# The first ten microseconds of an encoder layer: how x and the first weights are fetched, and what runs meanwhile

## The chip, the core and the metric

The kernel runs on one core of a Trainium2 chip. A core has engines that work side by side, each through its own list of instructions in order: TensorE (PE in the profile, its weight loads PEld), VectorE (DVE), ScalarE (ACT), GpSimd (POOL) and SyncE (SP). Data come from HBM into the core's SBUF by DMA; here SP and ACT issue transfers, each onto a queue of its own, and 16 DMA engines serve both. The matmuls' results go to PSUM. The metric is the device time of one execution in microseconds, as the median of several runs.

## What is computed

One layer of a hybrid encoder over 256 tokens of 1024 features, in float32: a half feed-forward step, a mixer (attention beside a state space model) and a second half step. Only the beginning of the first half step matters here.

```python
def rmsnorm(x, g):
    xf = x.astype(jnp.float32)
    y = xf * lax.rsqrt(jnp.mean(xf * xf, axis=-1, keepdims=True) + EPS)
    return (y * g).astype(x.dtype)

def swiglu(h, w_gate, w_up, w_down):
    return (jax.nn.silu(h @ w_gate) * (h @ w_up)) @ w_down

x = x + 0.5 * swiglu(rmsnorm(x, ffn1_norm[l]), ffn1_w_gate[l], ffn1_w_up[l], ffn1_w_down[l])
...
x = x + 0.5 * swiglu(rmsnorm(x, ffn2_norm[l]), ffn2_w_gate[l], ffn2_w_up[l], ffn2_w_down[l])
```

`w_gate` and `w_up` are 1024 x 2816, `w_down` is 2816 x 1024.

## The kernel before

x lies in SBUF as 8 tiles of 128 features by 256 tokens. To keep float32 precision with the faster matmul type, every operand is split in two: `hi` is the value rounded to that type (a copy on ACT, L94), and `lo` is the rest (a subtraction on DVE, L97, or L100 where a gain is multiplied in). A product then takes three matmuls: `hi` by `hi`, `hi` weights by `lo` activations, `lo` weights by `hi` activations (`mm3`, L136 to L138).

The half step (`ffn`) runs over 22 blocks of 128 hidden features. A block has 1 MB of weights, half gate and half up, and 2 x 8 x 3 = 48 matmuls of 128x128 weights by 128x256 activations. `wload` fetches weights into one of four `raw` buffers of 512 KB by SP's queue (L117), splits them into `whi` and `wlo` (four buffers each), and lets the splits run ahead of other work by a priority of 50. A planner sorts the instructions of each engine by readiness and priority; after that each engine keeps its order. It gives each transfer one of a fixed set of semaphores, and a transfer whose semaphore is still in use waits on its issuing engine.

The normalisation's factor per token (`R`) is not needed before the matmuls: x times the gain goes in (`Norm.scale`, which writes `xh` and `xl`), and `R` is multiplied in as a block's sum leaves PSUM. `Norm.square` collects the squares of x, and `Norm.finish` makes `R` with two small matmuls, one of which needs the identity matrix in `cst`. PSUM has six buffers for the blocks' sums.

The beginning, in the order of the queues: ACT issues the packed vectors `vec` (with the gains, L165) and then x[2:4] and x[4:8] (L167, L168); SP issues x[0:2] (L166), and behind it block 0's weights in four quarters of 256 KB, then the constants `cst` (L351), the positions and the packed rows (L293, L294), and the weights of block 1. Block 0 is a case of its own: its quarters are split without priority, and its matmuls run gate first (all 8 tiles of x), then up. `hook(f)` is called in each block: at 0 it issues `cst` and makes the squares, at 3 it makes the rotary tables, later it fetches the first weights of the mixer.

Of the kernel before, what the change touches and what calls it, by code (L numbers as in the profile page):

```python
# [15 lines left out]
P = 128  # L16
# [6 lines left out]

# pool depths
RAWB, WB = 4, 4
NMM, NPL, NG = 3, 2, 3
EB, PRB, QKB = 4, 2, 2
# blocks of the first half step during which the mixer's first weights are fetched
PREF = (8, 10, 12, 14, 16, 18)
# how far the splitting of weights runs ahead of other work  # L30
WPRI = 50
# emission order of the mixer, in rounds (one round per group of the state space part):
# attention units, state space units, its norm, weight chunks
A0, DA = -0.0991, 0.1594
# [13 lines left out]

# columns of the packed per-feature vectors
V_F1, V_MIX, V_F2, V_QA, V_KVA, V_SSM, V_DSK, V_CW, V_CB = 0, 8, 16, 24, 27, 29, 45, 61, 181  # L50
V_N = 205
# columns of the packed per-column rows
R_DTB, R_AL, R_GQ, R_GK, R_IF = 0, 64, 128, 224, 320
R_N = 336
# columns of the constant matrices
C_ID, C_TF, C_TB, C_S1, C_S2 = 0, 128, 256, 384, 448
# [16 lines left out]
def build(ctx, tc, A, out, dbg=None):  # L73
# [17 lines left out]

# [1 line left out]
    def copy(dst, src, scale=1.0):  # L93
        S.activation(dst, src, AF.Copy, scale=scale)  # L94

    def tt(dst, a, b, op):
        V.tensor_tensor(out=dst, in0=a, in1=b, op=op)  # L97

# [28 lines left out]
    def split(hi, lo, src, scale=None):  # L127
        if scale is None:
            copy(hi, src)
            tt(lo, src, hi, ALU.subtract)  # L130
        else:
            copy(hi, src, scale)
            stt(lo, src, scale, hi, ALU.mult, ALU.subtract)
# [6 lines left out]
    def wstat(ps, pieces, xh, xl, k0, first, last):  # L140
        """ps[feature, token] += sum over the k tiles held in pieces"""
        ks = [(pc, j) for pc, j0, n in pieces for j in range(j0, j0 + n)]
        for i, (pc, j) in enumerate(ks):
            mm3(ps, pc.hi[:, j * P:(j + 1) * P], pc.lo[:, j * P:(j + 1) * P],
                xh[:, k0 + i], xl[:, k0 + i], first and i == 0, last and i == len(ks) - 1)

    def rsqrt(y, v, n):
        """y = v ** -0.5 on [P, n]"""
        t = sm.tile([P, 8], I32, tag="rs_t", name="rs_t")[:, :n]
        a = sm.tile([P, 8], F32, tag="rs_a", name="rs_a")[:, :n]  # L150
        w = sm.tile([P, 8], F32, tag="rs_w", name="rs_w")[:, :n]
        ts(t, v.bitcast(I32), 1, None, ALU.logical_shift_right)
        ts(y.bitcast(I32), t, -1.0, float(0x5F3759DF), ALU.mult, ALU.add)
        ts(w, v, -0.5, None, ALU.mult)
        for _ in range(3):
            tt(a, y, y, ALU.mult)
            tt(a, a, w, ALU.mult)
            stt(y, a, 1.5, y, ALU.add, ALU.mult)

# [1 line left out]
    vec = cp.tile([P, V_N], F32, name="vec")  # L161
    row = cp.tile([P, R_N], F32, name="row")
    cst = cp.tile([P, C_N], F32, name="cst")
    x = xp.tile([P, KD, T], F32, name="x")
    nc.scalar.dma_start(vec, A["vec"])  # L165
    nc.sync.dma_start(x[:, 0:2], A["xt"][:, 0:2])  # L166
    nc.scalar.dma_start(x[:, 2:4], A["xt"][:, 2:4])  # L167
    nc.scalar.dma_start(x[:, 4:8], A["xt"][:, 4:8])  # L168
    ident = cst[:, C_ID:C_ID + P]
    triF = cst[:, C_TF:C_TF + P]  # L170
    triB = cst[:, C_TB:C_TB + P]
    ones = cp.tile([P, P], F32, name="ones")
    V.memset(ones, 1.0)
    halfpi = cp.tile([P, 1], F32, name="halfpi")
    V.memset(halfpi, PI / 2)

    def token_sums(psp, sq, tag):
        """[token, 2]: the sum of sq[feature, token] over its features"""
        ps = psp.tile([P, 512], F32, tag=tag, name="ps_sum")
        for t in range(2):  # L180
            TE.matmul(ps[:, t:t + 1], sq[:, t * P:(t + 1) * P], ones[:, 0:1], start=True, stop=True)
        return ps[:, 0:2]

    def token_rows(psp, r, tag):
        """[P, token]: r[token, 2] on every partition"""
        dg = sm.tile([P, 2, P], F32, tag="diag", name="diag", bufs=1)
# [18 lines left out]
    class Norm:  # L205
        """x * gain of each tile of x as it comes, and the sum of squares"""

# [27 lines left out]

# [1 line left out]
    def ffn(norm, wgu, wd, after, hook=None):  # L237
        with ExitStack() as es:
# [6 lines left out]
            R = None  # L245
            for f in range(KF):
                ps = ps_mm.tile([P, 2, T], F32, tag="mm", name="ps_gu")
                if f == 0 and hook:
                    pcs = wload(wgu[f], [512], 0)
                    for k in range(KD):  # L250
                        norm.scale(k)
                    pcs += wload(wgu[f, :, 512:2048], [512] * 3, 0)
                    for j in range(2):
                        wstat(ps[:, j], [(pcs[2 * j], 0, 4), (pcs[2 * j + 1], 0, 4)], norm.xh, norm.xl, 0, True, True)
                else:
                    pcs = wload(wgu[f], [1024, 1024])
                    for j in range(2):
                        wstat(ps[:, j], [(pcs[j], 0, KD)], norm.xh, norm.xl, 0, True, True)
                if hook:
                    hook(f)  # L260
                if R is None:
                    R = norm.finish(ps_r, "r")
                gu = ev.tile([P, 2, T], F32, tag="gu", name="gu")
                tt(gu, ps, R.unsqueeze(1).to_broadcast([P, 2, T]), ALU.mult)
                sg = ev.tile([P, T], F32, tag="sg", name="sg")
                S.activation(sg, gu[:, 0], AF.Silu)
                tt(sg, sg, gu[:, 1], ALU.mult)
                split(hh[:, f], hl[:, f], sg)
            for d in range(KD):
                ps = ps_mm.tile([P, 2, T], F32, tag="mm", name="ps_d")  # L270
# [5 lines left out]

# [1 line left out]
    CCq = cp.tile([P, 2, ROPE], F32, name="CCq")  # L278
# [11 lines left out]
    def tables():  # L290
# [6 lines left out]
        V.tensor_copy(eye, ident)  # L297
        # 0 where a pair of tokens counts, -2**100 elsewhere
        ts(msk4[:, 0], ones, 1.0, 2.0 ** 100, ALU.subtract, ALU.mult)
# [42 lines left out]

# [1 line left out]
    n1 = Norm(V_F1)  # L344
# [3 lines left out]

    def hook(f):
        if f == 0:  # L350
            nc.sync.dma_start(cst, A["cst"])  # L351
            for k in range(KD):
                n1.square(k)
        elif f == 3:
            tables()
        elif f in PREF:
# [7 lines left out]

# [1 line left out]
    with ExitStack() as es:  # L366
# [9 lines left out]

# [1 line left out]
        cqh = mp.tile([P, 3, T], F32R, name="cqh")  # L378
# [50 lines left out]

        # rotated shared key and its square sum  # L430
        H = ROPE // 2
# [10 lines left out]

        # dt = softplus(raw + bias), log-decay sums
        u = m0.tile([P, 2, 64], F32, name="dt_u")
# [20 lines left out]
        dump("dt", dt)  # L465
        # log-decay sums counted from the middle of the sequence outwards
        sgt = m0.tile([P, 2, P], F32, name="sgt")
# [36 lines left out]

# [1 line left out]
        def in_group(g):  # L506
# [30 lines left out]

# [1 line left out]
        def attn_group(g):  # L539
            st = {}  # L540

            def proj():
# [4 lines left out]
                for t in range(2):  # L547
# [14 lines left out]
                    copy(kv[:, t], pk, rk[:, t:t + 1])  # L562
                # head norms
                sq = at.tile([P, 512], F32, tag="pr", name="sq", bufs=PRB)[:, :2 * HG * HD].rearrange("p (t h d) -> p t h d", t=2, h=HG)
# [9 lines left out]
                rsqrt(r.rearrange("p a b c -> p (a b c)"), v.rearrange("p a b c -> p (a b c)"), 4 * HG)  # L574
                # rotary part of q, in place
                qr = q4[:, :, :, NOPE:]
# [5 lines left out]
                tt(qr, qr, m2, ALU.add)  # L582
                # k
                ka = at.tile([P, 2, HG, HD], F32, tag="ka", name="ka", bufs=1)
# [52 lines left out]

# [1 line left out]
        def ssd_group(g, xz):  # L639
# [122 lines left out]

# [1 line left out]
        for c in range(4):  # L764
# [24 lines left out]

# [1 line left out]
    ffn(n2, A["w_gu2"], A["w_d2"], lambda d: nc.sync.dma_start(out[:, d], x[:, d]))  # L791


# [1 line left out]
def _tiles(w):  # L795
    """[K, M] -> [M tiles, partition, K tiles, 128]"""
    k, m = w.shape
    return w.reshape(k // P, P, m // P, P).transpose(2, 1, 0, 3)


def _pairs(t):
    """[n, P, K, 128] -> [n / 2, P, 2 * K * 128]"""
    n, p, k, m = t.shape
# [88 lines left out]
```

## Time and profile before

| what | value |
|---|---|
| time, median of 3 runs | 819.84 us (818.7 to 819.92) |
| span of the profiled execution, first to last instruction | 817.6 us |
| TensorE busy in the span | 797.8 us, 6480 matmuls |
| first matmul of block 0 | 7.34 us |
| bytes moved by DMA | 126.61 MB |
| weights of a block, issue to landing | 4.5 us (median of 86 pieces of 512 KB) |
| block 0's quarters, issue to landing | 6.8 us (median of 4 pieces of 256 KB) |

The times are of runs without the profiler; the profile is of one execution, of which it gives the span alone. All stamps below are microseconds from the start of that span. In a row of the timeline the first number is the start and the second the duration of the group, and "x4" counts its instructions. Matmuls are pipelined, so the duration of one is longer than the distance to the next; that distance is what a matmul costs in a row of them.

### The profile page before, as it was taken

How to read it: one execution, taken by the hardware profiler on the slowest of the kernel's cores; microseconds unless marked ns; L12 is line 12 of the kernel's file. 1: busy time of each engine (PE TensorE's matmuls, PEld its weight loads, DVE VectorE, ACT ScalarE, POOL GpSimd, SP SyncE). 2: the span in 40 equal slices, each digit the busy share in tenths (PEclk: the TensorE clock that was granted, in tenths of full speed). 3: DMA queues.
4: the chain of work that ended last, by engine and by line, in shares of the span. 5: the costliest groups of instructions: out<-in, count | busy, mean ns of one | idle time of the engine just before them, and what ended most of it. 6: DMA issues, size and time to landing. Idle time of an engine off the chain costs nothing.

```text
span 817.6 us, 16082 instructions
## 1 busy us (share of the span) xinstructions
PE 797.8 (98%) x6480; PEld 768.8 (94%) x6480; DVE 590.3 (72%) x1192; ACT 470.2 (58%) x810; POOL 0.2 (0%) x4
## 2 busy tenths in 40 slices
PE   6999999999998999999999999999999999999998
PEld 5999999999998998988989999999999999999998
DVE  6977776566797986897897578657787766666543
ACT  6755554455367659679676666557455544444342
POOL 0000000000000000000000000000000000000000
PEclk9999999999999999999999999999999999999999
DMA  7667774667235443322325414342665555554772
GB/s 259 214 212 224 222 229 136 184 184 215 63 92 171 131 131 104 106 79 92 103 85 168 154 52 154 112 146 68 223 184 178 175 184 182 185 184 131 197 206 75
DMA packets 39098, 126.61 MB, mean 155 GB/s; under 512 B 4464, under 2 KB 5872, under 8 KB 39024
## 3 DMA queue, kind: packets, MB, share of 16 engines
q1 hardware_dynamic: 38592, 124.69, 48.7%
q8 instruction: 51, 0.84, 0.4%
q10 hardware_dynamic: 432, 0.89, 0.3%
q14 instruction: 23, 0.19, 0.1%
HBM read 124.52 MB, written 1.05 MB: 154 GB/s over the span
## 4 chain that ended last, share of the span: by engine, by line
PE 86%; DVE 6%; ACT 5%; DMA 2%; issue 1%; ACTq 0%
PE ps_gu L137 10%; PE ps_gu L138 10%; PE ps_gu L136 10%; PE ps_d L136 5%; PE ps_d L137 5%; PE ps_d L138 5%; PE ps_in L137 4%; PE ps_in L138 4%; PE ps_in L136 4%; PE ps_y L690 3%; PE ps_sb L138 2%; PE ps_sb L137 2%; PE ps_sb L136 2%; PE ps_sc L603 2%; PE ps_gt L137 1%; PE ps_o L630 1%
## 5 line engine op out<-in xcount | busy, mean ns | idle before, releaser
L94 ACT ACTIVATE whi<-raw 128x1024 fp32r<-128x1024 f32 (+4 forms) x256 | 251.3, 986 | 209.0 <-PE ps_d L137 53.1
L97 DVE TENSOR_TENSOR wlo<-raw,whi 128x1024 fp32r<-128x1024 f32 (+4 forms) x256 | 289.8, 1134 | 112.1 <-ACT whi L94 111.2
L136 PE MATMUL ps_gu<-xh,whi 128*128 128x256 f32 x704 | 201.0, 285 | 7.9 <-ACT whi L94 7.9
L137 PE MATMUL ps_gu<-xl,whi 128*128 128x256 f32 x704 | 201.2, 286 | 0.5 <-DVE xl L100 0.4
L138 PE MATMUL ps_gu<-xh,wlo 128*128 128x256 f32 x704 | 200.8, 285 | 0.0
L136 PEld LDWEIGHTS ps_gu<-xh,whi 128*128 128x128 f32 x704 | 136.5, 194 | 8.2 <-ACT whi L94 8.2
L137 PEld LDWEIGHTS ps_gu<-xl,whi 128*128 128x128 f32 x704 | 136.5, 194 | 1.0 <-DVE xl L100 0.9
L138 PEld LDWEIGHTS ps_gu<-xh,wlo 128*128 128x128 f32 x704 | 136.4, 194 | 0.5 <-DVE wlo L97 0.5
L137 PE MATMUL ps_in<-xl,whi 128*128 128x256 f32 x368 | 105.3, 286 | 0.1
L138 PE MATMUL ps_in<-xh,wlo 128*128 128x256 f32 x368 | 105.0, 285 | 0.0
L136 PE MATMUL ps_in<-xh,whi 128*128 128x256 f32 x368 | 104.4, 284 | 0.0
L137 PE MATMUL ps_d<-hl,whi 128*128 128x256 f32 x352 | 99.1, 281 | 0.0
L136 PE MATMUL ps_d<-hh,whi 128*128 128x256 f32 x352 | 99.1, 281 | 0.0
L138 PE MATMUL ps_d<-hh,wlo 128*128 128x256 f32 x352 | 99.0, 281 | 0.0
L137 PEld LDWEIGHTS ps_in<-xl,whi 128*128 128x128 f32 x368 | 70.1, 191 | 0.6 <-DVE xl L100 0.3
L138 PEld LDWEIGHTS ps_in<-xh,wlo 128*128 128x128 f32 x368 | 70.1, 191 | 0.5 <-issue 0.3
L136 PEld LDWEIGHTS ps_in<-xh,whi 128*128 128x128 f32 x368 | 70.1, 191 | 0.1
L136 PEld LDWEIGHTS ps_d<-hh,whi 128*128 128x128 f32 x352 | 66.3, 188 | 0.0
L137 PEld LDWEIGHTS ps_d<-hl,whi 128*128 128x128 f32 x352 | 66.3, 188 | 0.0
L138 PEld LDWEIGHTS ps_d<-hh,wlo 128*128 128x128 f32 x352 | 66.3, 188 | 0.0
L100 DVE SCALAR_TENSOR_TENSOR xz<-ps_in,vec,xz 128x254 f32<-128x254 f32 (+1 forms) x96 | 44.8, 476 | 1.6 <-ACT xz L520 0.9
L94 ACT ACTIVATE hh<-sg 128x256 fp32r<-128x256 f32 x44 | 18.1, 415 | 45.9 <-DVE sg L97 45.9
(222 smaller groups left out, 1467.5 us busy)
## 6 DMA issues: line engine op xcount, KB each, us to landing
raw<-in_w_gu SPq DMA_DIRECT2D x86, 512.0 KB, 4.5
raw<-in_w_in SPq DMA_DIRECT2D x62, 512.0 KB, 4.4
raw<-in_w_d SPq DMA_DIRECT2D x32, 384.0 KB, 3.2
raw<-in_w_d SPq DMA_DIRECT2D x32, 320.0 KB, 3.4
raw<-in_w_sb SPq DMA_DIRECT2D x16, 512.0 KB, 4.4
raw<-in_w_qkv SPq DMA_DIRECT2D x8, 544.0 KB, 3.8
raw<-in_w_ab SPq DMA_DIRECT2D x8, 512.0 KB, 3.8
raw<-in_w_o SPq DMA_DIRECT2D x8, 512.0 KB, 4.2
```

Source lines behind the costliest of these rows:

```text
L94: S.activation(dst, src, AF.Copy, scale=scale)
L97: V.tensor_tensor(out=dst, in0=a, in1=b, op=op)
L100: V.scalar_tensor_tensor(out=dst, in0=a, scalar=s, in1=b, op0=op0, op1=op1)
L136: TE.matmul(ps, whi, xhi, start=first, stop=False)
L137: TE.matmul(ps, whi, xlo, start=False, stop=False)
L138: TE.matmul(ps, wlo, xhi, start=False, stop=last)
L603: TE.matmul(sc[:, t * T:(t + 1) * T], qk[:HD, t * P:(t + 1) * P], qk[:HD, T:2 * T], start=True, stop=True)
L630: TE.matmul(po[64 * j:64 * j + 64, :T], kv[:, kt, HG * NOPE + hh_ * 64:HG * NOPE + (hh_ + 1) * 64], st[hh_][:, kt], start=kt == 0, stop=kt ...
L690: TE.matmul(py[64 * j:64 * j + 64, a:b], st[c, d][:, hh_], M[i][:, j, a:b], start=n == 0, stop=n == 3)
```

## The change

Before anything else x and block 0's weights are issued, each in three pieces that go together: tiles 0 and 1 of x with the columns of the weights that meet them, then tiles 2 and 3, then 4 to 7. x goes by SP's queue, the weights by ACT's, behind `vec`. The weights go into `w0`, which has the place of an `xh` buffer that is free then. ACT makes one copy of a constant (`idle`), which brings its table load forward. TensorE begins with ten matmuls of `ones` by `ones` (float32, 128x128). Block 0 (`block0`) splits and multiplies piece by piece, gate and up in turn, into two PSUM buffers in place of one. Its sum is multiplied by `R` only after block 1, in two instructions. `cst` is issued in block 1, after that block's weights, and the work of `tables()` on each engine may not pass the last subtraction of block 0's split. The comments are taken out of the file.

```diff
+STEPS = (0, 2, 4, 8)
+NWARM = 10
...
     def split(hi, lo, src, scale=None):
         if scale is None:
             copy(hi, src)
-            tt(lo, src, hi, ALU.subtract)
+            return tt(lo, src, hi, ALU.subtract)
...
-    nc.scalar.dma_start(vec, A["vec"])
-    nc.sync.dma_start(x[:, 0:2], A["xt"][:, 0:2])
-    nc.scalar.dma_start(x[:, 2:4], A["xt"][:, 2:4])
-    nc.scalar.dma_start(x[:, 4:8], A["xt"][:, 4:8])
+    with tc.high_priority(1000):
+        nc.scalar.dma_start(vec, A["vec"])
+    w0 = xnp.tile([P, KD, T], F32, tag="xh", name="w0").rearrange("p (j a) b -> p j (a b)", j=2)
+    for k, e in zip(STEPS, STEPS[1:]):
+        with tc.high_priority(1000):
+            nc.sync.dma_start(x[:, k:e], A["xt"][:, k:e])
+            nc.scalar.dma_start(w0[:, :, k * P:e * P], A["w_gu1"][0].rearrange("p (j a) -> p j a", j=2)[:, :, k * P:e * P])
...
+    idle = cp.tile([P, 1], F32, name="idle")
+    with tc.high_priority(500):
+        S.activation(idle, ones[:, 0:1], AF.Copy)
...
+    begun = []
+
+    def block0(ps_mm, ps_r, norm):
+
+        warm = ps_r.tile([P, 512], F32, tag="r", name="warm")
+        for _ in range(NWARM):
+            TE.matmul(warm[:, :P], ones, ones, start=True, stop=True)
+        pss = [ps_mm.tile([P, 2, T], F32, tag="mm", name="ps_gu0")[:, 0] for _ in range(2)]
+        w = [(wp.tile([P, 1088], F32R, tag="whi", name="whi"), wp.tile([P, 1088], F32R, tag="wlo", name="wlo"))
+             for _ in range(2)]
+        for k, e in zip(STEPS, STEPS[1:]):
+            c = slice(k * P, e * P)
+            with tc.high_priority(500):
+                norm.scale(k)
+                for j in range(2):
+                    begun[:] = [split(w[j][0][:, c], w[j][1][:, c], w0[:, j, c])]
+                    if j == 0:
+                        for m in range(k + 1, e):
+                            norm.scale(m)
+            for j in range(2):
+                for m in range(k, e):
+                    s = slice(m * P, (m + 1) * P)
+                    mm3(pss[j], w[j][0][:, s], w[j][1][:, s], norm.xh[:, m], norm.xl[:, m], m == 0, m == KD - 1)
+        return pss
...
-            for f in range(KF):
-                ps = ps_mm.tile([P, 2, T], F32, tag="mm", name="ps_gu")
-                if f == 0 and hook:
-                    pcs = wload(wgu[f], [512], 0)
-                    for k in range(KD):
-                        norm.scale(k)
-                    pcs += wload(wgu[f, :, 512:2048], [512] * 3, 0)
+
+            def evict(f, pss):
+                gu = ev.tile([P, 2, T], F32, tag="gu", name="gu")
+                if len(pss) == 2:
                     for j in range(2):
-                        wstat(ps[:, j], [(pcs[2 * j], 0, 4), (pcs[2 * j + 1], 0, 4)], norm.xh, norm.xl, 0, True, True)
+                        tt(gu[:, j], pss[j], R, ALU.mult)
                 else:
...
+            todo = []
+            for f in range(KF):
+                if f == 0 and hook:
+                    todo.append((f, block0(ps_mm, ps_r, norm)))
+                else:
+                    ps = ps_mm.tile([P, 2, T], F32, tag="mm", name="ps_gu")
+                    pcs = wload(wgu[f], [1024, 1024])
+                    for j in range(2):
+                        wstat(ps[:, j], [(pcs[j], 0, KD)], norm.xh, norm.xl, 0, True, True)
+                    todo.append((f, (ps,)))
+                if hook:
+                    hook(f)
+                if f == 0 and hook:
+                    continue
+                if R is None:
+                    R = norm.finish(ps_r, "r")
+                for t in todo:
+                    evict(*t)
+                todo = []
...
     def hook(f):
+        if f == 1:
+            nc.sync.dma_start(cst, A["cst"])
         if f == 0:
-            nc.sync.dma_start(cst, A["cst"])
             for k in range(KD):
                 n1.square(k)
         elif f == 3:
-            tables()
+            with tc.issue_after(begun[0].ins):
+                tables()
```

More of the change, by code (lines that the diff above doesn't have):

```diff
@@ L96, in tt @@
     def tt(dst, a, b, op):
-        V.tensor_tensor(out=dst, in0=a, in1=b, op=op)
+        return V.tensor_tensor(out=dst, in0=a, in1=b, op=op)
     def stt(dst, a, s, b, op0, op1):
@@ L245, in ffn @@
             R = None
-            for f in range(KF):
-                ps = ps_mm.tile([P, 2, T], F32, tag="mm", name="ps_gu")
-                if f == 0 and hook:
-                    pcs = wload(wgu[f], [512], 0)
-                    for k in range(KD):
-                        norm.scale(k)
-                    pcs += wload(wgu[f, :, 512:2048], [512] * 3, 0)
+            def evict(f, pss):
+                gu = ev.tile([P, 2, T], F32, tag="gu", name="gu")
+                if len(pss) == 2:
                     for j in range(2):
-                        wstat(ps[:, j], [(pcs[2 * j], 0, 4), (pcs[2 * j + 1], 0, 4)], norm.xh, norm.xl, 0, True, True)
+                        tt(gu[:, j], pss[j], R, ALU.mult)
                 else:
[L256 to L264, printed above, removed]
+                    tt(gu, pss[0], R.unsqueeze(1).to_broadcast([P, 2, T]), ALU.mult)
                 sg = ev.tile([P, T], F32, tag="sg", name="sg")
```

## The prediction

> **What bounds the kernel now.** I read the page's first two sections, then the busy time by stages, then PE's waits and the start of the timeline, and last the DMA queues.
>
> ```profile
> span 817.6 us, 16082 instructions
> PE 797.8 (98%) x6480; PEld 768.8 (94%) x6480; DVE 590.3 (72%) x1192; ACT 470.2 (58%) x810; POOL 0.2 (0%) x4
> ...
> 7.34:11.16 3.82, 3.23 (x12) 2.71 (x12) 3.59 (x10) 3.42 (x9) 0.00 (x0) 1.00 1.04 390
> 11.16:15.26 4.10, 4.09 (x17) 3.87 (x18) 3.87 (x11) 2.98 (x7) 0.00 (x0) 1.00 0.59 128
> 15.26:20.00 4.74, 4.74 (x40) 4.74 (x40) 3.47 (x13) 3.07 (x6) 0.00 (x0) 1.00 0.89 342
> ...
> 40.00:60.00 20.00, 20.00 (x169) 20.00 (x169) 14.84 (x19) 10.54 (x16) 0.00 (x0) 1.00 0.63 208
> ...
> PE ps_gu L136 <- ACT whi L94: 7.9, 2, 7.3
> ```
>
> In a stage row stand the stretch, its length, then the busy time of PE, PEld, DVE, ACT and POOL, the granted clock, the DMA share and GB/s. TensorE is busy 797.8 of 817.6 us, and from 15 us on it has no hole until the mixer. Up to 130 us its only listed wait is 7.9 us for `whi`: 7.3 us before its first matmul and 0.6 us later. So the end moves by what the beginning moves, no more.
>
> The beginning has a second cost, which the waits don't show. Matmuls of one shape start at two spacings:
>
> ```profile
> 14.41 0.41 PE L137 MATMUL ps_gu<-xl,whi 128*128 128x256 f32 x1
> 14.62 0.41 PE L138 MATMUL ps_gu<-xh,wlo 128*128 128x256 f32 x1
> ...
> 15.45 0.29 PE L136 MATMUL ps_gu<-xh,whi 128*128 128x256 f32 x1
> 15.57 0.28 PE L137 MATMUL ps_gu<-xl,whi 128*128 128x256 f32 x1
> 15.69 0.28 PE L138 MATMUL ps_gu<-xh,wlo 128*128 128x256 f32 x1
> ```
>
> Until 15.4 us one takes 0.21 us (14.41 to 14.62), afterwards 0.12 us. The granted clock says 1.00 throughout, so this slow start is to be read from spacings alone. Block 0 has 2 x 8 x 3 = 48 matmuls; the one at 15.45 is the 31st. It ends at 15.45 + 18 x 0.12 = 17.6 us; at full speed a block takes 48 x 0.12 = 5.76 us. I give each version a **head**: the end of block 0 less 5.76 us, the moment at which a TensorE that never waits and is never slow would have begun. Before, the head is 11.85 us. The change is worth the difference of heads, if nothing later starves.
>
> **Part by part.** (1) *Table load and constant matmuls.* The table load no longer waits for x, but ACT will wait for data anyway, so it is worth nothing by itself.
>
> ```profile
> 4.97 1.28 ACT L94 ACT_TABLE_LOAD   x1 [4.97 <-DMA x<-in_xt]
> ...
> 6.68 0.61 ACT L94 ACTIVATE whi<-raw 128x512 fp32r<-128x512 f32 x1
> 7.20 1.29 ACT L94 ACTIVATE xh<-x,vec 128x256 fp32r<-128x256 f32 x3
> 7.32 0.69 DVE L97 TENSOR_TENSOR wlo<-raw,whi 128x512 fp32r<-128x512 f32 x1
> ...
> 8.07 0.58 PE L138 MATMUL ps_gu<-xh,wlo 128*128 128x256 f32 x1
> ...
> 11.17 0.58 PE L136 MATMUL ps_gu<-xh,whi 128*128 128x256 f32 x1 [0.60 <-ACT whi L94]
> ...
> 31.15 0.70 PE L190 MATMUL ps_rows<-diag,ones 128*128 128x256 f32 x2
> ...
> 416.72 1.03 PE L646 MATMUL ps_cb<-xz 128*128 128x256 f32 x4
> 417.59 1.04 PE L654 MATMUL ps_xT<-cst,xz 128*128 128x128 f32 x8
> ```
>
> A plain float32 matmul is recorded as two (one call at L190 gives x2). At 128x256 two calls take 417.59 - 416.72 = 0.87 us, 0.43 us each at full speed; at 128x128 half of that, 0.22, and slow at 0.21/0.12 of it, 0.39. Ten are some 4 us, on a TensorE that has nothing else to do: from 1.1 to about 5 us. Do they lift the speed? The trace has one rise: at 15.4 us, 4.2 us after the unbroken stretch began at 11.17. The 3 us stretch from 7.34 did not do it. Four microseconds lie between, so this is a toss-up.
>
> On that, the Trainium skill ("TensorE: Matmul & The Clock Gate", Part 1) says that a free-running window of about 3.4 us must be busy for the full clock, and one must be idle to lose it. The rise 4.2 us after 11.17 agrees; by it about 4 us of constants hold a whole window in less than a third of runs, and that is the slow rival below.
>
> (2) *The transfers.* This is where I think the change loses what it aims at. Before, all that block 0 needs, and nothing else, stands first in both queues. After, seven transfers carry it (ACT: the vectors and three pieces of the weights; SP: x in three), and SP goes on at once with the 512 KB pieces of block 1.
>
> ```profile
> 0.00:2.00 2.00, 0.00 (x0) 0.00 (x0) 0.54 (x4) 0.00 (x0) 0.20 (x4) 1.00 0.06 11
> 2.00:4.00 2.00, 0.00 (x0) 0.00 (x0) 0.00 (x0) 0.00 (x0) 0.00 (x0) 1.00 0.83 156
> 4.00:9.00 5.00, 1.66 (x6) 1.43 (x7) 2.16 (x5) 3.62 (x7) 0.00 (x0) 1.00 1.00 380
> 9.00:11.20 2.20, 1.60 (x9) 1.31 (x7) 1.97 (x7) 2.20 (x6) 0.00 (x0) 1.00 1.05 392
> ...
> q10 hardware_dynamic: 94, 0.39, 68.1%
> q1 hardware_dynamic: 94, 0.16, 30.1%
> ...
> x<-in_xt ACTq DMA_DIRECT2D x1, 512.0 KB, 7.2
> ...
> x<-in_xt ACTq DMA_DIRECT2D x1, 256.0 KB, 5.1
> ...
> vec<-in_vec ACTq DMA_DIRECT2D x1, 102.5 KB, 4.4
> ...
> 1.16 0.46 ACTq L167 DMA_DIRECT2D x<-in_xt  x1
> 1.17 2.12 SPq L117 DMA_DIRECT2D raw<-in_w_gu  x4
> 1.65 0.45 ACTq L168 DMA_DIRECT2D x<-in_xt  x1
> ...
> SPq L351 <- DMA vec<-in_vec: 1.8, 1, 1.8
> ```
>
> The q rows are those of 6 to 7.5 us, with both queues full: ACT's queue (q10) moved 94 packets, and SP's (q1) 94. They share by packets, not by bytes: 0.39 against 0.16 MB, since one of q10 held 4 KB and one of q1 2 KB. A packet is one run of one partition. After, ACT's weight pieces have runs of 1, 1 and 2 KB (sixteen of them to each of the 16 DMA engines), while SP has 2 and 4 KB runs, eight to an engine and transfer. Now ACT is the loser. Counting packets of one engine: the vectors (8) and the first piece (16) end with SP's 24 of x, when 0.105 + 0.262 + 1.049 = 1.42 MB have gone. The second piece (16) ends with both halves of block 1, after 1.42 + 0.26 + 1.05 = 2.73 MB. The third (16) ends with the constants and a half of block 2, after 2.73 + 0.52 + 0.25 + 0.52 = 4.02 MB. Does SP have these queued in time? Eight transfers were issued before the constants at L351 waited for the vectors' landing, so eight can be open: the first half of block 1 is the eighth, the second goes out when the vectors land (0.72 + 4.4 = 5.1 us), the constants next, and block 2 when the first weights have landed, 3 us ahead of its turn.
>
> The rows above give 0.02 MB by 2 us, 0.33 by 4, 2.24 by 9, then 0.39 per us. So the three pieces are moved at 6.9, 10.2 and 13.5 us. From there to the landing, the same count of before's own pieces of x on ACT's queue gives 5.5 and 7.5 us, and they landed at 1.16 + 5.1 = 6.3 and 1.65 + 7.2 = 8.9: add 0.8 to 1.4. I take 7.8, 11.1 and **14.5 us**. Before, block 0 waited for no data after 11.17.
>
> The Trainium skill ("DMA: Bandwidth & Descriptors", Queues, rings and completion order) says that an engine alternates between queue rows packet by packet, and that a packet typically holds 9 to 17 descriptors. The 94 against 94 agree with turns; were each whole piece one turn, the second would come with x and the third with block 1, which is one of the cases of the fast rival.
>
> (3) *From the last landing to the end of block 0.* A 512-wide `whi` gave its first matmul 7.34 - 6.68 = 0.66 us after it began, its `wlo` 8.07 - 6.68 = 1.39. So the third piece's first matmul starts at 15.2, gate's `wlo` serves from 15.9, and ten more end at 17.1. Up's `whi` stands behind three `xh` (1.29 us for 3), if the scheduler keeps the order written: it starts at 14.5 + 0.53 + 1.29 = 16.3, `wlo` serves from 17.7, end 18.9; with the `xh` done earlier 18.55. At full speed the head is 12.8 to 13.1, against 11.85: **+1.2 us**.
>
> (4) *What is only moved.* The constants are wanted by `diag`, and block 0 now holds two PSUM buffers of six, so the first eviction must come before block 5, at 13 + 5 x 5.76 = 41.8 us:
>
> ```profile
> 30.61 0.48 DVE L104 TENSOR_SCALAR diag<-cst,nr 128x128 f32<-128x128 f32 x2
> ...
> 31.89 0.39 ACT L94 ACTIVATE R<-ps_rows 128x256 f32<-128x256 f32 x1 [0.91 <-PE ps_rows L190]
> ```
>
> The constants land by about 14.5 us, 16 us ahead of `diag`, and `R` came 10 us ahead of that limit; were this cover gone, PE would wait microsecond for microsecond. The rotary tables now stand behind the last `wlo` of block 0 on DVE; the mixer reads them after 200 us. Behind that `wlo` comes block 1's own, 1.2 us, ready as PE arrives at 18.9: no loss, no slack. Behind SP's waiting ninth transfer are only constants and block 2. The split of one eviction in two is 0.1 us off the path. Sum of these: nothing.
>
> **The rivals.** *Slow: the speed does not rise early.* If neither the constants nor the broken bursts from 7.8 and 11.1 us lift it, the last 24 matmuls start at 15.2 at 0.21 us. Speed comes 4.2 us later, as after 11.17, at 19.4, with 20 done: head 19.4 - 44 x 0.12 = 14.1, +2.3 us. With 3 us it is +1.8; with the 8.1 us that passed from 7.34 to 15.4, +4.0. Against it: some 4 us of constants, then 12 matmuls per piece. For it: idle from about 5 to 7.8 us, longer than any hole that this trace shows without a loss. Then the matmuls on constants don't do what they are for. It decides if no rise comes before 15 us.
>
> *Fast: the weights are not held up.* If the queues share by bytes here, the third piece lands when 2 x 1.13 MB have gone, at 9.1 + 0.8 = 9.9 us, and part (3) ends 4.6 us earlier: -3.4 us at full speed; slow until 12 us (an unbroken run from 7.9), head 12.1 - 20 x 0.12 = 9.7, -2.1. With turns of whole pieces the third lands at 11, some -2. Against it stand the equal counts.
>
> **Numbers.** The span is 817.6 us, the runs' median 819.84, so 2.2 us lie around the span; the runs reach from 818.7 to 819.92, as the moment of the rise could explain. Forecast: late weights, full speed by 15 us, 819.84 + 1.2 = **821.0** (820.2 to 821.7), chance 0.43. Slow rival: 822.1 (821.6 to 823.8), 0.33. Fast rival: 817.3 (816.4 to 818.3), 0.22. The last 0.02 is no net effect. About 0.2%, 1.64 us, can be told from no change. Beyond 821.5 lie most of the slow rival and an edge of the forecast, 0.37; below 818.2 nearly all of the fast one, 0.20; same 0.43. The range 817.0 to 823.0 takes the forecast, nine tenths of the slow rival and the upper part of the fast one.
>
> **What would show it.** The landing of the three pieces in the DMA view (7.8, 11.1, 14.5 us); the packets of q10 against q1 between 8 and 13 us; holes of PE before the second and third burst; spacing 0.21 or 0.12 at the first real matmul and at 15 us; end of block 0 near 18.8. A third piece landing before 11 us makes the forecast wrong at part (2), a spacing of 0.21 after 15.2 at part (1), a PE hole between 19 and 45 us at part (4).

## The result and the profile after

The changed kernel takes 825.57 us in the median (825.46 to 827.91), the kernel before 819.88 beside it (818.7 to 820.03): a ratio of 1.0076, 95% interval 1.0053 to 1.0099. It is slower by 5.7 us, where 1.2 were forecast, and outside the range. The profiled execution took 825.46 us, with a span of 823.7.

First the stages of the changed kernel, with the columns of the rows shown of before (stretch, length, busy time of PE, PEld, DVE, ACT, POOL, granted clock, DMA share, GB/s):

```profile
span 823.7 us, 16121 instructions
...
4.00:9.00 5.00, 1.45 (x8) 1.25 (x7) 0.48 (x1) 1.17 (x3) 0.00 (x0) 0.95 1.00 361
9.00:11.20 2.20, 0.00 (x0) 0.00 (x0) 0.00 (x0) 0.00 (x0) 0.00 (x0) 0.50 1.00 393
11.20:16.00 4.80, 1.62 (x7) 1.62 (x8) 1.64 (x5) 2.09 (x6) 0.00 (x0) 0.50 0.86 326
16.00:20.00 4.00, 4.00 (x26) 4.00 (x25) 4.00 (x12) 4.00 (x10) 0.00 (x0) 0.66 0.00 0
...
33.40:40.00 6.60, 5.39 (x42) 4.97 (x41) 6.05 (x35) 3.84 (x5) 0.00 (x0) 1.00 0.52 175
```

The clock column shows 1.00 as long as a profile has no clock record yet. The first record of the kernel before is at 15.39 us, that of the changed kernel at 5.07, so the 1.00 ahead of them says nothing of the speed: from 11.98 to 15.39 us before, 16 matmuls are counted, in the next 3.41 us 30.

The DMA engines are full and TensorE, VectorE and ScalarE stand still from 9 to 11.2 us, where before TensorE was busy 1.60 of 2.20 us. The starts of PE's work say where it waits, in the timeline of the changed kernel:

```profile
1.04 4.40 PE L254 MATMUL warm<-ones 128*128 128x128 f32 x20 [1.04 <-DVE halfpi L186]
14.38 0.58 PE L140 MATMUL ps_gu<-xh,whi 128*128 128x256 f32 x1 [8.93 <-ACT whi L98]
...
18.91 0.28 PE L140 MATMUL ps_gu<-xh,whi 128*128 128x256 f32 x1
19.03 0.28 PE L141 MATMUL ps_gu<-xl,whi 128*128 128x256 f32 x1
...
22.14 0.28 PE L140 MATMUL ps_gu<-xh,whi 128*128 128x256 f32 x1
...
33.42 0.28 PE L141 MATMUL ps_gu<-xl,whi 128*128 128x256 f32 x1
34.67 0.61 PE L192 MATMUL ps_sum<-ones,nacc 128*128 128x1 f32 x4 [0.97 <-DVE nacc L101]
...
209.39 0.39 PE L140 MATMUL ps_in<-xh,whi 128*128 128x256 f32 x1 [0.90 <-DVE x L104]
```

There are no three bursts from 7.8, 11.1 and 14.5 us on. TensorE idles for 8.93 us and all of block 0 runs in one go from 14.38. Its 49th matmul, the first of block 1, starts at 22.14, so the head is 22.14 - 5.76 = 16.38 us. These are the rows of the kernel before:

```profile
17.60 0.28 PE L136 MATMUL ps_gu<-xh,whi 128*128 128x256 f32 x1
...
25.88 0.28 PE L136 MATMUL ps_gu<-xh,whi 128*128 128x256 f32 x1
26.18 0.61 PE L181 MATMUL ps_sum<-ones,nacc 128*128 128x1 f32 x4
...
202.57 0.28 PE L136 MATMUL ps_in<-xh,whi 128*128 128x256 f32 x1
```

Its 49th starts at 17.60, which makes a head of 11.84 (the prediction's 11.85 comes from rounded spacings): +4.54. Two holes follow that before had not, or not so large: in front of `ps_sum` (33.42 to 34.67, some 1.1 us more than the 0.12 of a matmul; before, 25.88 to 26.18) and of the first `ps_in` (0.90 us; before, no wait). The last addition of the squares on VectorE, which `ps_sum` waits for, is 8.5 us later, in the kernel before and then in the changed one:

```profile
25.70 0.42 DVE L97 TENSOR_TENSOR nacc<-nacc,nsq 128x256 f32<-128x256 f32 x1
...
34.20 0.42 DVE L101 TENSOR_TENSOR nacc<-nacc,nsq 128x256 f32<-128x256 f32 x1
```

Why the first matmul is so late is told by the order of the transfers. These are rows of the DMA view of the changed kernel, one group each for the windows up to 1.7 us, from 1.7 to 2.2, and from 2.2 to 3.2 (KB each, us from issue to landing; a transfer whose issue spans two windows is shown once):

```profile
w<-in_w_gu ACTq DMA_DIRECT2D x1, 256.0 KB, 6.6
vec<-in_vec ACTq DMA_DIRECT2D x1, 102.5 KB, 3.9
...
w<-in_w_gu ACTq DMA_DIRECT2D x1, 512.0 KB, 9.6
raw<-in_w_gu SPq DMA_DIRECT2D x1, 512.0 KB, 8.2
x<-in_xt SPq DMA_DIRECT2D x1, 256.0 KB, 6.2
...
w<-in_w_gu ACTq DMA_DIRECT2D x1, 256.0 KB, 11.4
```

The text issues 256, 256 and 512 KB; the queue got 256, 512 and 256. So the largest, piece 3, went second. By the offsets in the built program the order is piece 2, piece 3, piece 1; the trace has no offsets, but agrees: the pieces land at 7.77, 11.42 and 13.89 us, and the first split in ScalarE's order, that of piece 1, starts right behind the last of them, with everything else waiting behind it:

```profile
4.68 0.50 ACT L98 ACTIVATE xh<-x,vec 128x256 fp32r<-128x256 f32 x1
13.91 0.42 ACT L98 ACTIVATE whi<-w 128x256 fp32r<-128x256 f32 x1 [8.72 <-DMA w<-in_w_gu]
```

The three landings are those forecast (7.8, 11.1, 14.5), only of other pieces. Where the sum goes, from the starts of the same instructions in both traces (the head as above; then from the 49th matmul of `ps_gu` to the 241st, to the first `ps_d`, to the first `ps_in`, and to the last matmul), in us:

| kernel (profiled execution) | head | 49th to 241st | to `ps_d` | `ps_d` to `ps_in` | `ps_in` to the last |
|---|---|---|---|---|---|
| before | 11.84 | 24.39 | 97.92 | 62.66 | 611.27 |
| after | 16.38 | 25.61 | 97.92 | 63.72 | 610.69 |
| difference | +4.54 | +1.22 | 0 | +1.06 | -0.58 |

The differences add up to 6.24 us; the spans differ by 6.1. The last column, 0.58 us less, is within what it varies between the profiles of this case (610.3 to 611.5). So there were three things to explain: the late head, the hole at `ps_sum`, and the hole at the mixer's start.

### The profile page after: what moved, and what is told of

Same layout as the page of the kernel before. It is cut to its first block, busy times and chain, and to the rows that moved or that the text cites. A ratio compares the mean times of both kernels' runs of the same rounds, so it can differ in the third digit from the quotient of the medians.

```text
span 823.7 us, 16121 instructions
## 1 busy us (share of the span) xinstructions
PE 800.6 (97%) x6500; PEld 772.2 (94%) x6500; DVE 589.0 (72%) x1195; ACT 469.9 (57%) x813; POOL 0.2 (0%) x4
## 4 chain that ended last, share of the span: by engine, by line
PE 83%; DVE 7%; ACT 5%; DMA 3%; issue 1%; ACTq 0%; SPq 0%
PE ps_gu L141 9%; PE ps_gu L142 9%; PE ps_gu L140 9%; PE ps_d L140 5%; PE ps_d L141 5%; PE ps_d L142 5%; PE ps_in L141 4%; PE ps_in L142 4%; PE ps_in L140 4%; PE ps_y L737 3%; DVE wlo L101 2%; PE ps_sb L142 2%; PE ps_sb L141 2%; PE ps_sb L140 2%; PE ps_sc L650 2%; PE ps_gt L141 1%
## 5 line engine op out<-in xcount | busy, mean ns | idle before, releaser
L101 DVE TENSOR_TENSOR wlo<-raw,whi 128x1024 fp32r<-128x1024 f32 (+1 forms) x252 | 286.9, 1139 | 111.2 <-ACT whi L98 109.8
L98 ACT ACTIVATE whi<-raw 128x1024 fp32r<-128x1024 f32 (+1 forms) x252 | 248.1, 991 | 201.2 <-PE ps_d L141 54.3
```

Source lines behind the costliest of these rows:

```text
L101: return V.tensor_tensor(out=dst, in0=a, in1=b, op=op)
```

## The experiments

All times are medians, beside runs of the kernel before on the same chip (819.44, 819.64 and 819.52 us in three groups of runs); ratios are against those. Heads and stretches are of one profiled execution each and worked out as above. Kernels with the same beginning differ in the head by up to 1.2 us: 9.60 to 10.83 in the four with weights on SP's queue, the text's order and no constants, 16.38 and 16.92 in the two with the beginning of the change. A difference of heads below that isn't shown.

**The order of the text.** The three blocks of priority join that of `vec`:

```diff
-    w0 = xnp.tile(...)
-    for k, e in zip(STEPS, STEPS[1:]):
-        with tc.high_priority(1000):
+        w0 = xnp.tile(...)
+        for k, e in zip(STEPS, STEPS[1:]):
```

> The changed kernel with one thing different: the seven first transfers are issued in the order of the text (pieces 1, 2, 3 of the weights; tiles 0-1, 2-3, 4-7 of x), where the changed kernel issued pieces 2, 3, 1 and tiles 0-1, 4-7, 2-3. Theory A (the order alone cost the time; the queues share well enough): the third piece lands by about 10 us, first matmul near 8, head 8.3 to 9.8, time 816.5 to 818. Theory B (the order cost a part, and block 1's 4 KB packets on SP's queue still hold the weights up): pieces land near 7.7, 11.1 and 14.0 us, head 12.8 to 14.1 against 16.4 in the changed kernel, time 821 to 823. Theory C (the order doesn't matter): time 825.5 as before.

The pieces land at 7.53, 11.05 and 14.15 us, in the text's order, and TensorE works in three bursts, as forecast. The timeline of this kernel shows their first matmuls:

```profile
8.02 0.39 PE L140 MATMUL ps_gu<-xh,whi 128*128 128x256 f32 x1 [2.35 <-ACT whi L98]
...
11.54 0.58 PE L140 MATMUL ps_gu<-xh,whi 128*128 128x256 f32 x1 [1.18 <-ACT whi L98]
...
14.86 0.58 PE L140 MATMUL ps_gu<-xh,whi 128*128 128x256 f32 x1 [0.35 <-ACT whi L98]
```

The head is 14.36, so order alone is worth 2.0 us of it in the profiled executions, about what theory B has (its head: 12.8 to 14.1). The time doesn't follow: 827.1 us (823.0 to 827.78), ratio 1.0075 (1.005 to 1.01). Two of its five runs took 823.0 and 823.2, the other three 827.1 to 827.8. The profiled one took 823.0, 2.5 us below the change; what the other three lost is in no trace and stays open, so that the gain of the order alone isn't shown in the time.

**The queues exchanged, the planner's order kept.** In the loop of the first transfers, weights go by SP and x by ACT:

```diff
-            nc.sync.dma_start(x[:, k:e], ...)
-            nc.scalar.dma_start(w0[:, :, k * P:e * P], ...)
+            nc.scalar.dma_start(x[:, k:e], ...)
+            nc.sync.dma_start(w0[:, :, k * P:e * P], ...)
```

> The change with one edit: weights on SP's queue, vectors and x on ACT's; the three blocks of priority stay, and with them an order of issue other than the text's (weights 1, 3, 2; x 2-3, 4-7, 0-1). Theory A (weights with short runs lose the shared DMA engines to x and block 1 with long ones): with the weights ahead of block 1 in their own queue, all seven pieces land by about 11 us instead of 13.9; x 0-1 last of its queue at about 9 us, first matmul near 9.5 us instead of 14.4, head 10.5 (11.5 if slow until the rise) instead of 16.4, and the time 825.6 less 5 to 6, plus or minus one: 819.5 to 821.5. Theory B (the order of issue alone is the loss, the queues share bytes fairly): the late first x takes the place of the late first weights, landing at 11 to 13 us; head 14 or more, time 823 to 825.

822.49 us (821.48 to 826.9), ratio 1.0043 (1.0024 to 1.0062); head 13.25. All seven pieces have landed by 10.65 us, as theory A had it, but x[0:2], the last issued of its queue, comes at 10.39 and not at 9, and the first matmul waits for its `xh`, in the timeline of this kernel:

```profile
11.03 0.58 PE L140 MATMUL ps_gu<-xh,whi 128*128 128x256 f32 x1 [5.51 <-ACT xh L98]
```

The gain is 3.1 us, in the head and in the time, between what A (5 to 6) and B (0.6 to 2.6) forecast: the late weights go, and a late x takes part of their place.

**Both.**

> Order of the text, and the queues exchanged: block 0's weights on SP's queue, so that block 1 stands behind them, and the vectors and x on ACT's. Theory B: nothing that block 0 doesn't need goes before 2.25 MB are moved; the last piece lands near 9.9 us, head 8.3 at full speed and 9.8 if TensorE is slow until about 12 us, time 816.3 to 818. Theory A: no better than e1_order, within 0.5 us. In both the wait for the sum of squares near 33 us is gone or below 0.5 us, as block 1 and the squares start earlier.

Head 10.34 us, 822.01 us (820.22 to 823.56), ratio 1.0027 (1.0017 to 1.0037). Neither theory had this: B's head (8.3 to 9.8) and time (816.3 to 818) are missed, and the wait for the sum of squares, which was to fall below 0.5 us, is 1.9. The four heads make a square:

| head, us | weights on ACT | weights on SP |
|---|---|---|
| planner's order | 16.38 | 13.25 |
| text's order | 14.36 | 10.34 |

The order is worth 2.0 and 2.9 us, the queue 3.1 and 4.0; together they bring the head 1.5 us below that of before. How the queues shared is seen in the DMA queues from 8 to 13 us (packets, MB, share of 16 engines), first in the change:

```profile
q1 hardware_dynamic: 462, 1.41, 72.0%
q10 hardware_dynamic: 425, 0.55, 31.0%
```

then with the queues exchanged and the text's order:

```profile
q1 hardware_dynamic: 609, 1.72, 86.0%
q10 hardware_dynamic: 103, 0.35, 17.3%
```

In the change SP (q1) and ACT (q10) moved nearly equally many packets, 462 and 425, but 1.41 and 0.55 MB: the short runs of the weights lost. Exchanged, ACT's queue has only the rest of x left after 8 us (0.35 MB, the last of it landing at 11.18), and the weights come first in SP's own order. Equal counts are no general rule, though. With the queues exchanged, both were loaded from 3 to 8 us:

```profile
q10 hardware_dynamic: 328, 0.70, 53.6%
q1 hardware_dynamic: 507, 0.61, 43.6%
```

Here the bytes are nearer to equal than the packets. Why the two mixes share differently is open.

And yet the kernel is 2.6 us slower than before. Its waits of PE (us in total, times, longest):

```profile
PE ps_sum L191 <- DVE nacc L101: 1.9, 1, 1.9
...
PE ps_in L140 <- DVE x L104: 0.9, 1, 0.9
```

The better head has run into both holes, the one at `ps_sum` larger than in the change: the stretch from the 49th matmul to the 241st takes 26.68 us instead of 24.39, that to `ps_in` 63.72 instead of 62.66.

**The matmuls on constants taken out of it.** `NWARM = 0`.

> e3_both without the ten matmuls on constants. If they are what lifts TensorE's speed, matmuls start at 0.21 us apart here and go on so for 3.4 to 6.8 us from the first unbroken stretch, 1.5 to 2 us slower than e3_both. If the speed that they gain is lost again before the first real matmul, or never gained, the two are equal within 0.5 us.

820.78 us (819.86 to 822.58), ratio 1.0015 (1.0004 to 1.0027), head 9.95: without them it is no slower, but 1.2 us faster in the median, where equal within 0.5 was the nearer expectation; the intervals of the ratios overlap. With the constants the clock was at 1.0 from 5.64 us without a break through block 0, without them from 10.95 on. So the speed that they gain was not lost here, and still gave nothing: block 0's last pieces land at 11.18 and 11.31 us with them, at 10.61 and 10.79 without. **Out of the change itself**, the same edit:

> The change without its matmuls on constants. Theory A (their speed was lost by 8.5 us, so they give nothing): speed rises 3.4 to 6.8 us after the first matmul at 14.4, at 17.8 to 21.2 us; head 15.9 to 17.4, time 825 to 826.5, no difference to the change that stands out of its runs. Theory B (even the short stretch of full speed helps the later rise): head 17 or more in every run, time 826.5 or more.

825.11 us (824.42 to 826.16), ratio 1.007 (1.0056 to 1.0084), head 15.93, the rise at 17.87 us. In the change they give nothing, as theory A said. **In the kernel before**, ten of them alone:

```diff
+            if hook:
+                warm = ps_r.tile([P, 512], F32, tag="r", name="warm")
+                for _ in range(10):
+                    TE.matmul(warm[:, :P], ones, ones, start=True, stop=True)
             for f in range(KF):
```

> The kernel before with the ten matmuls on constants added and nothing else. If the speed that they gain lasts over the idle stretch from 5.4 to 7.3 us, all matmuls are 0.12 us apart from the first, block 0 is bound by its last weights (36 matmuls from 11.2 us on): head 9.7 against 11.85, time 817.7, 2.1 us less than before. If it doesn't last, 819.9 as before.

820.0 us (819.31 to 822.99), ratio 1.0011 (1.0001 to 1.002), head 12.19. The 2.1 us didn't come. The windows of this kernel show why:

```profile
6.81:10.22 3.41, 3.16 (x12) 2.71 (x12) 2.48 (x6) 2.34 (x7) 0.00 (x0) 1.00 1.03 357
10.22:13.63 3.41, 1.92 (x14) 1.65 (x14) 3.41 (x10) 3.21 (x6) 0.00 (x0) 1.00 0.42 140
13.63:17.04 3.41, 3.41 (x18) 3.41 (x18) 3.13 (x13) 1.81 (x6) 0.00 (x0) 0.50 0.93 273
```

The first record of full clock begins only at 10.22 us (the 1.00 in the first row is a column without a record), so in this execution the constants, done by 5.7 us, had raised nothing; and full clock is taken away at 13.63 for 3.41 us, in which 18 matmuls are counted instead of some 28. **Enough constants to last until the data come**, in the change: `NWARM = 44`.

> The change with 44 matmuls on constants instead of 10, so that TensorE stays busy from 1 us to 13 or 14 us, just before its first weights. Theory A (the ten raised the speed at 5 us, and the idle time until 14.4 us lost it again, so that the first 20 to 24 matmuls of block 0 ran at 0.21 us each): the granted clock is 1.0 without a break from 5 to 8 us on, spacing 0.12 at the first real matmul, head 16.4 less about 2: 14.4, time 823.6. Theory B (the spacing at the start is that of data, not of speed, or the clock drops all the same): head 16 to 16.5, time 825.6.

The clock is held: 1.0 from 6.77 to 30.67 us, and 57 matmuls stand in the 8 us from 13.94, first in this timeline the last constants and then block 0:

```profile
1.04 12.81 PE L254 MATMUL warm<-ones 128*128 128x128 f32 x88 [1.04 <-DVE halfpi L186]
13.94 0.39 PE L140 MATMUL ps_gu<-xh,whi 128*128 128x256 f32 x1
...
31.96 1.02 PE L192 MATMUL ps_sum<-ones,nacc 128*128 128x1 f32 x4 [5.09 <-DVE nacc L101]
```

The head falls to 15.04, by 1.35 us of the 2 expected. But the time is 830.65 us (ratio 1.0136, 1.0117 to 1.0155), 5 us worse than the change, which neither theory named: with the longer row of constants the planner puts `ps_sum` on PE behind 96 matmuls of `ps_gu` (before 118, change 143), and TensorE waits 5.09 us there for the squares. That hole then costs the clock too: 0.5 from 30.67 to 37.49 us.

**The sum of squares later.** To the version of both, without constants, one edit: `finish` behind the first half of block 3.

```diff
-                if f == 0 and hook:
+                if f < 3 and hook:
                     continue
-                if R is None:
+                if R is None and hook:
+                    with tc.issue_after(half[0].ins):
+                        R = norm.finish(ps_r, "r")
+                elif R is None:
```

> e4 with one edit: the sum of squares is finished behind block 3 of gate/up instead of as early as the order allows; ps_sum then stands on PE after 192 matmuls of ps_gu instead of 143. Theory A (the hole of 2.3 us at 27.1 us in e4 is TensorE waiting at ps_sum for the squares' sum, which VectorE finishes late): the hole shrinks to what its own four matmuls and two of ps_rows take, about 1.0 us; the head counted at the 240th matmul falls from 13.0 to about 11.8, and the time from 820.8 to 819.5. Theory B (VectorE or ScalarE is simply behind by then, whatever stands where): a hole of the same size appears elsewhere before the 240th matmul, time as e4, 820.8. If the sum is asked for too late, block 5 waits for a PSUM buffer: a hole near 38 us.

The wait is gone, and the stretch to the 241st matmul falls from 26.09 to 24.45 us: theory A. 818.22 us (817.8 to 819.23), ratio 0.9983 (0.9974 to 0.9992), 2.6 us better. That is more than the stretch gained, but the two profiled executions lie on opposite sides of their medians (820.24 and 819.23 us) and differ by 1.0 only; the head of this one was 0.9 later.

**The mixer's PSUM groups exchanged.** To the version of both, without constants, the other edit:

```diff
-        ps_mm = es.enter_context(pool("ps_mm", NMM, ...))
         ps_pl = es.enter_context(pool("ps_pl", ...))
+        ps_mm = es.enter_context(pool("ps_mm", NMM, ...))
```

> e4 with one edit: the two groups of PSUM buffers of the mixer are laid out in the exchanged order, so that its first tile ps_in0 doesn't follow the last ps_d tile in the same bank. Theory A (the one buffer more that block 0 uses shifted the rotation, and the first ps_in matmul waits for the last eviction out of the same bank): the listed wait of ps_in for x, 0.9 us, is gone, the stretch from the first ps_d to the first ps_in falls from 63.7 to 62.7 us, and the time from 820.8 to 819.8. Theory B (the mixer waits for x itself, its input, whatever the bank): the wait stays at 0.9 to 1.0 us and the time at 820.8.

`ps_in` no longer stands in the list of waits, and `ps_d` to `ps_in` takes 62.66 us, to the digit that of before: theory A. 819.95 us (819.42 to 820.56), ratio 1.0 (0.9991 to 1.0009), 0.8 us better. In its profiled execution the hole at `ps_sum` took the clock along (0.5 from 30.33 to 33.74 us), which hides the gain there: the stretch to the 241st matmul is 27.52 us, 1.4 more than without the edit.

**Both edits in the changed kernel alone:**

> The changed kernel with the two hole edits alone (sum of squares behind block 3, PSUM groups exchanged); queues, order of issue and the matmuls on constants as in the change. Theory A (of the 5.7 to 6 us that the change cost, about 4.5 are the head and the rest the two holes): the head stays at 16.4, the two holes go, and the time falls from 825.6 to about 823.5. Theory B (the late weights are the whole cost, and what follows only shifts): 825.6 as the change.

823.73 us (823.63 to 826.28), ratio 1.0053 (1.0038 to 1.0067): 1.8 us of the loss are gone. The stretches are 24.04 and 62.66 us, and the head (16.92) is no better.

**All together:** queues exchanged, the text's order, no constants, sum later, PSUM groups exchanged.

> e4 with both of these edits: queues exchanged, the text's order of issue, no matmuls on constants, sum of squares behind block 3, PSUM groups exchanged. Theory A (head and the two holes are the whole difference to before): head 9.95 against 11.85 and no hole more than before, so 1.9 us under before: 817.6 when before is at 819.5. Theory B (the mixer or the last stages have a wait of their own that takes it back, or the holes move): 819 to 820.5, no difference to before.

817.19 us (817.13 to 818.21), ratio 0.9968 (0.9956 to 0.9981): faster than both kernels. Its rows of the same stages:

```profile
span 815.4 us, 16080 instructions
...
4.00:9.00 5.00, 2.50 (x11) 2.45 (x12) 1.79 (x5) 2.59 (x9) 0.00 (x0) 1.00 0.98 311
9.00:11.80 2.80, 2.80 (x15) 2.80 (x14) 1.46 (x5) 1.43 (x5) 0.00 (x0) 1.00 1.03 406
11.80:16.00 4.20, 3.82 (x27) 3.24 (x27) 4.17 (x11) 4.20 (x9) 0.00 (x0) 1.00 0.92 361
...
33.00:40.00 7.00, 6.86 (x56) 6.60 (x56) 6.52 (x21) 3.47 (x4) 0.00 (x0) 1.00 0.73 224
```

TensorE is busy from 9 to 11.8 us throughout (at 0.21 us a matmul until the rise at 11.77), and from 33 to 40 us the hole is 0.14 us. Head 10.24, then 24.46 and 62.66 us: 1.6 us are won at the head and none given back before `ps_in`; the rest up to the spans' 2.2 us is behind `ps_in`, a stretch that differs by half a microsecond between executions anyway.

**And constants until its data come:** `NWARM = 15`.

> e8 with 15 matmuls on constants, enough to keep TensorE busy until its first data at 6.5 us. Theory A (block 0 there is set by the landing of the last pieces at about 11.2 us, whose 24 matmuls run at full speed anyway): the clock is 1.0 from 5 to 8 us on, but the head stays at 10.0 to 10.4 and the time at 817.2, as e8. Theory B (the slow matmuls before the rise at 11.8 us cost up to 2 us of the head): head 9 or less, time 816.

Full clock from 4.55 us without a break, yet head 10.55 and 818.31 us (817.41 to 820.07), ratio 0.9986 (0.9977 to 0.9995). The head is nearer to theory A's 10.0 to 10.4 than to B's 9: the last pieces of weights and x land at 10.54 and 11.41 us (11.27 and 11.09 in the version without constants), and half of block 0's matmuls have to come after them, so full speed from the first matmul on doesn't help. The time is 1.1 us worse than without, which A didn't say; 0.5 us of it stand between the 49th and 241st matmul, and the rest isn't settled.

## Why the prediction was wrong

- **What bounds the kernel: right.** The difference is made before 45 us, plus one hole at the mixer's start, the place up to which the prediction itself saw PE without a hole. From the 241st matmul to `ps_d` not a hundredth changed.
- **Part (2), "ACT is the loser": right.** The landings are 7.53, 11.05 and 14.15 us with the text's order against 7.8, 11.1 and 14.5, and in the change the packets are nearly equal (462 to 425). Exchanging the queues gives 3.1 to 4.0 us of head. "They share by packets, not by bytes" holds for this mix and not as a rule: with the queues exchanged it is 507 to 328 packets, 0.61 to 0.70 MB. The Trainium skill ("DMA: Bandwidth & Descriptors", Queues, rings and completion order) has an engine take turns between queue rows, packet by packet. The counts of the change agree with turns of equally many runs, those with the queues exchanged don't.
- **Part (2), the step that failed:** "The second piece (16) ends with both halves of block 1 ... The third (16) ends with the constants" takes the pieces in the order of the text. The change wraps each pair of transfers in a priority block of its own, and the planner, which sorts by readiness and priority, issued weights 2, 3, 1. So block 0 didn't start with the first landing and end soon after the last, it started with the last. With the text's order the bursts and landings are those of the forecast. This is 2.0 us of the head (16.38 to 14.36).
- **Part (1), a toss-up that fell as the slow rival, the second step that failed:** the forecast took "full speed by 15 us". The ten constants did raise the clock (1.0 from 5.07 us), and the idle time lost it (0.5 from 8.49 until 18.73; with the text's order from 9.46 until 19.70). With the text's order the head was 14.36 us; the slow rival's was 14.1, the forecast's 12.8 to 13.1, so the lost clock is some 1.3 to 1.6 us of it by difference, little more than heads of the same beginning differ by. The slow rival was right in size and in the late rise (19.4 us), not in that the speed never rises earlier; it had 0.33 of the chance. How much of the head is contention and how much clock was not run apart with this order; in the planner's order holding the clock gave 1.35. The remark that the granted clock "says 1.00 throughout" read a column without records: the first, at 15.39 us, is where the spacing changes.
- **Part (4), "Sum of these: nothing", the third step that failed, by 2.3 us** (1.22 + 1.06), of which taking both holes away gave back 1.8 in the time. The covers that it named did hold: constants, `R` and tables came in time. What it left out was on PE's own order. The squares start at 20.88 us on ScalarE (before, 13.37), behind the splits of block 0 and block 1, and the last of their additions on VectorE is 8.5 us later than before. `ps_sum` has a fixed place among the matmuls, behind 143 of them, whose turn came at 33.5 us, so TensorE waits for it; giving it a later place removed the wait. And "two PSUM buffers of six" was weighed only for block 5's wait. The 22 blocks and 8 `ps_d` take 30 buffers before, five rounds of six, and 31 after, so by this count the last `ps_d` is in the first buffer, where the mixer begins. That the place of the buffers makes the wait is shown by the exchange; that block 0's second buffer moved it is by count, not by a run of its own.
- **The rival on the other side:** the fast one (queues that share by bytes) is refuted for the change by 1.41 against 0.55 MB. That its head, 9.7 with a late rise, is about what the weights on SP's queue reach (9.95) is chance: they go there ahead of block 1, in one queue with it.

The whole: 2.0 us by order, 2.5 by the rest of the head (contention and lost clock, which the slow rival put at 2.3), 2.3 by two holes, less 0.6 behind `ps_in`, gives 6.2 in the trace and 5.7 in the medians. Block 0's work in pieces, the copy that brings the table load forward and the moved tables were not run by themselves.

## What to carry to other kernels

Check in the built order, or in the landings by size, that the first transfers go out in the order in which they are needed: priority blocks of their own let a planner reorder them, and the one needed first may land last. Where two queues share the engines and the bulk in the other has longer runs, put what is needed first ahead of the bulk in the same queue (here 3.1 and 4.0 us of head). Faster matmuls ahead of the last landing give nothing if half of the work has to come after it. A gain at the start is only kept if what stands at fixed places further on comes earlier too: after each shift, read the waits of the bottleneck engine up to the end of the next stage, and count PSUM buffers over the whole rotation.

## What the runs showed of the hardware

The granted clock changes in steps of 3.41 us, and full clock is taken away after a step in which TensorE was far from idle. Two rows for each of two versions, the step that decides and the one after it. The mixer's PSUM groups exchanged:

```profile
26.92:30.33 3.41, 1.69 (x15) 1.54 (x14) 2.75 (x14) 2.34 (x2) 0.00 (x0) 1.00 0.51 180
30.33:33.74 3.41, 3.41 (x18) 3.41 (x18) 3.28 (x21) 0.55 (x2) 0.00 (x0) 0.50 0.44 150
```

Queues exchanged and the text's order, with constants:

```profile
26.12:29.53 3.41, 1.70 (x15) 1.49 (x13) 3.24 (x12) 2.99 (x5) 0.00 (x0) 1.00 0.78 251
29.53:32.95 3.42, 3.25 (x27) 3.25 (x28) 3.02 (x19) 0.91 (x1) 0.00 (x0) 1.00 0.50 169
```

With 1.69 us of work in the step the clock fell, with 1.70 it stayed. In the 14 profiles of this case, leaving out the steps in which a kernel ends, all eight steps at full clock with 1.69 us or less, from 0 up, were followed by a fall; of the 13 with 1.70 to 1.97 one was (the 1.92 quoted above, in the kernel before with ten constants, where no hole was longer than 1.3 us), and of those with more none. Of the steps in which a kernel ends, five held that little: three with 0.01 to 0.25 us were followed by a fall, two with 1.56 and 1.58 (queues exchanged with the text's order, and all together) were not within the span. So the clock is lost at about half a step of work here, with busy times that the profile models, but not at a sharp threshold. The Trainium skill ("TensorE: Matmul & The Clock Gate", Part 1) names an idle window of about 3.4 us as what loses it: the length agrees, the idleness doesn't. A step with little work is how the constants lost their clock in the change (0.38 us of work from 5.07 to 8.49) and with the text's order alone (1.44 from 6.05 to 9.46). With the weights on SP's queue as well, the steps behind them held 2.06 and 2.19 us, the clock stayed, and the constants were worth nothing because the data came late. Falls like these are also a part of the scatter between executions: in the version of both without constants the step from 256.72 us, in the mixer, held 1.54 us of work and cost the clock for one step, where in other executions the steps fell elsewhere and it stayed.
